# Power of the norms on few columns, low weight parts on VectorE, and operand sums of the weights kept in DRAM, in a hybrid decoder layer

## The chip, the cores and the metric

The kernel runs on one core of one Trainium2 chip. The metric is the device time of one execution in microseconds (us). In the rows of the profile PE is TensorE's matmuls, PEld its weight loads, DVE is VectorE, ACT ScalarE, POOL GpSimd, and SP (SPq) SyncE's queue, which here issues every DMA.

## The reference

One layer of a decoder runs over 2048 prompt tokens and 64 sample tokens. Two mixers (an S5 scan and an HGRN2 recurrence) give a row of 1024 numbers per token. What matters here comes behind them:

```python
def rmsnorm(x, g):
    xf = x.astype(jnp.float32)
    r = xf * lax.rsqrt(jnp.mean(xf * xf, axis=-1, keepdims=True) + EPS)
    return (r * g.astype(jnp.float32)).astype(x.dtype)
...
        x = x + jnp.concatenate([y5, yh], axis=-1) @ w_out[l]
        h2 = rmsnorm(x, norm_ffn[l])
        x = x + (jax.nn.silu(h2 @ w_gate[l]) * (h2 @ w_up[l])) @ w_down[l]
...
    y = rmsnorm(x, norm_final)
```

`w_out` is 1024 x 1024, `w_gate` and `w_up` are 1024 x 2816, `w_down` is 2816 x 1024, all in float32.

## The kernel before

The work falls into two parts. Up to about 842 us the mixers run (projections, the recurrence's heads, the scan, the gated unit). Behind that the 2112 tokens are taken in three blocks b = 0, 1, 2 of FT = 704, each in two halves of FH = 352: `mix` multiplies by `w_out` (matmuls into `pA_o`, `pB_o`, `pQ_o`), `norm2` normalises and stores the combinations of h that the next product needs, `ffn` runs the gate/up steps and then the down products, and `final` normalises the result and stores it. The order of the stages is mix 0, mix 1 with norm2 of block 0 in its middle, mix 2 with norm2 of block 1, norm2 of block 2, ffn 0, ffn 1 with the last norm of block 0 set behind its second step, ffn 2 with that of block 1, and the last norm of block 2 alone at the end. The norms are named f0, f1, f2 (`norm2`) and z0, z1, z2 (`final`).

Every large product is a two-by-two block product made with seven multiplications instead of eight, which `seven` issues. Each wants a sum of blocks of the weights as stationary data and one of the tokens as moving data. An operand is a float32 sum split in two parts, hi (its rounding, `wh`, `xh`) and lo (the rest, `wl`, `xl`), and three matmuls of 128 x 352 replace one: hi hi, lo hi, hi lo. So a gate/up step, which makes two pairs of blocks of 128 columns of gate and of up, is 7 products x 2 matrices x 12 = 168 matmuls. There are 11 such steps per block, and 6 groups of down products with 924 matmuls per block.

`w_prep` makes the weights' operands for one step: for each matrix it loads 1 MB in two DMAs of 512 KB into a raw tile `wr` (two of them exist), makes four sums of the four blocks on DVE (L1037, L1038, L1044, L1045), and for each of the seven operands lets ACT write hi (L1031) and POOL write lo (L1032). The seven operands go to a pool of ten slots, so a slot must be freed by the matmuls of an earlier operand. All weights are read and summed again in each of the three blocks.

A gate/up product ends in a sink: for gate `s` gets the product by ACT, or DVE adds a second product (L1105) and ACT takes SiLU; for up DVE adds (L1128) and multiplies `s` by `u` (L1129); the last up product is multiplied (L1119), DVE makes four combinations `T` (L976 to L979), and seven stores of 176 KB write `s_s`. The gate's last product (the seventh, at the 145th matmul of the step) goes to the bank of `pA_g`, and waits for L1105 to have read that bank.

`norm_r` squares eight tiles of 128 x 704 on ACT, adds them on DVE, sums over the partitions by a matmul with a matrix of ones (L1174), which gives each sum on all 128 partitions, scales on DVE (L1175), and raises to the power -1/2 on POOL over 128 x 704 (L1176). `norm2` and `final` then multiply on DVE (L1185, L1201).

The order of instructions on each engine is fixed when the program is built, by a scheduler that plans with its own costs. An engine runs its list in order, so an instruction that waits holds those behind it.

Of the kernel before, what the change touches and what calls it, by code (L numbers as in the profile page):

```python
# [265 lines left out]
def tiles_of(t0, n):  # L266
    r = []
    while n > 0:
        w = min(P, n)
# [20 lines left out]
        nc.gpsimd.tensor_tensor(r[:rows, a:b], st[:rows, a:b], e.mhalf[:rows, 0:b - a], op=ALU.pow)  # L290


def spread(e, r, tiles, name):
# [717 lines left out]
    return out  # L1011


def w_prep(e, mats, nk):
# [4 lines left out]
    out = [[] for _ in mats]
    gens = []  # L1020

    def prep(srcs, name, ops):
# [24 lines left out]
        sp(a12)
        yield
        sp(a21)
        yield  # L1050
        sp(a22)
        yield
# [403 lines left out]
```

## Time and profile before

| | |
|---|---|
| runs | 3363.42, 3372.87, 3374.15 us |
| median | 3372.87 us |
| profiled execution | 3370.24 us |
| its span, first to last instruction | 3368.5 us |
| granted TensorE clock, mean | 0.861 of full speed |
| PE, DVE, ACT, POOL busy | 2398.2, 2269.8, 996.7, 2300.7 us |

Three engines are busy for two thirds of the span, and none for all of it. So a share over the whole span does not say what holds the kernel; the stages have to be looked at one by one.

### The profile page before, as it was taken

To read this page: it belongs to the slowest core of one execution; us is meant where nothing else is said; L and a number is where in the kernel's file an instruction comes from. 1 tells how busy PE (TensorE), PEld (TensorE's weight loads), DVE (VectorE), ACT (ScalarE), POOL (GpSimd) and SP (SyncE) were. 2 spreads that over 40 slices of the span, in tenths; PEclk is the share of its full clock that TensorE was granted. 3 is DMA by queue.
4 is the path that set the end of the run, shared out by engine and by line. 5 is a ranking of instruction groups with operands and counts; after the bars stand their busy time and mean duration, and the time that the engine had idled before them with its cause. 6 is when DMAs were issued, how large, how long until landed. Compare 5 with 4: busy or idle time off the path is not lost.

```text
span 3368.5 us, 44865 instructions
## 1 busy us (share of the span) xinstructions
PE 2398.2 (71%) x16813; PEld 2210.8 (66%) x16813; DVE 2269.8 (67%) x2692; ACT 996.7 (30%) x1848; POOL 2300.7 (68%) x1587
## 2 busy tenths in 40 slices
PE   7989999997713705029999985298998816898840
PEld 6977677785703705029998985288988816898840
DVE  8754545455596896946678788667777795667730
ACT  4322222222301302004434442043434402344310
POOL 4176585511587698866667778976767797666778
PEclk9999999998856857559999998599999957999975
DMA  8865644545414704123324431142353204334300
GB/s 253 226 226 163 182 152 144 161 141 194 162 59 149 258 16 143 57 83 125 138 100 159 142 138 47 68 166 104 138 176 131 99 4 167 114 118 156 131 19 34
DMA packets 249323, 441.57 MB, mean 131 GB/s; under 512 B 80265, under 2 KB 165586, under 8 KB 249106
## 3 DMA queue, kind: packets, MB, share of 16 engines
q1 hardware_dynamic: 249106, 438.71, 39.1%
q8 instruction: 132, 2.16, 0.3%
q14 instruction: 85, 0.70, 0.1%
HBM read 314.86 MB, written 123.76 MB: 130 GB/s over the span
## 4 chain that ended last, share of the span: by engine, by line
PE 30%; DVE 21%; POOL 19%; DMA 12%; issue 10%; POOLq 3%; ACT 2%; SPq 1%; DVEq 0%; ACTq 0%
POOL rr_f L1176 7%; PE pA_u L1076 4%; POOLq L1448 3%; POOL rr_z L1176 3%; PE pA_g L1076 3%; DMA wr_u<-in_w_up_u 3%; PE pA_d L1076 3%; DVE ct L976 2%; DMA wr_wd<-in_w_down_u 2%; POOL wl_wd L1032 2%; PE ps_v L263 2%; PE ps_u L263 2%; DVE s L1129 2%; PE ps_f L263 1%; PE pQ_g L1076 1%
## 5 line engine op out<-in xcount | busy, mean ns | idle before, releaser
L1032 POOL TENSOR_TENSOR wl_u<-wr_u,wh_u 128x512 fp32r<-128x512 f32 x231 | 354.9, 1541 | 198.5 <-ACT wh_u L1031 154.6
L1032 POOL TENSOR_TENSOR wl_wd<-wr_wd,wh_wd 128x512 fp32r<-128x512 f32 (+1 forms) x252 | 382.7, 1545 | 151.9 <-ACT wh_wd L1031 137.8
L1032 POOL TENSOR_TENSOR wl_g<-wr_g,wh_g 128x512 fp32r<-128x512 f32 x231 | 353.0, 1531 | 140.4 <-ACT wh_g L1031 136.2
L1176 POOL TENSOR_TENSOR rr_z<-rr_z,mhalf 128x704 f32<-128x704 f32 x3 | 338.0, 112665 | 18.5 <-DVE rr_z L1175 18.5
L1176 POOL TENSOR_TENSOR rr_f<-rr_f,mhalf 128x704 f32<-128x704 f32 x3 | 337.9, 112625 | 10.9 <-DVE rr_f L1175 10.9
L1076 PE MATMUL pA_g<-xh_h,wh_g 128*128 128x352 f32 x528 | 186.1, 352 | 220.5 <-ACT s L1103 137.2
L1076 PEld LDWEIGHTS pA_g<-xh_h,wh_g 128*128 128x128 f32 x528 | 107.1, 203 | 231.7 <-ACT s L1103 138.1
L1076 PE MATMUL pA_g<-xh_h,wl_g 128*128 128x352 f32 x528 | 182.1, 345 | 98.8 <-POOL wl_g L1032 98.8
L1076 PE MATMUL pA_o<-xh_y,wh_wo 128*128 128x352 f32 x192 | 73.2, 385 | 247.3 <-ACT xh_y L1008 117.3
L1076 PE MATMUL pA_u<-xh_h,wh_u 128*128 128x352 f32 x528 | 178.7, 338 | 85.3 <-ACT u L1126 72.7
L1032 POOL TENSOR_TENSOR wl_wo<-wr_wo,wh_wo 128x512 fp32r<-128x512 f32 x84 | 143.1, 1731 | 109.2 <-ACT wh_wo L1031 100.2
L1076 PE MATMUL pA_d<-xh_s,wh_wd 128*128 128x352 f32 x528 | 179.7, 340 | 44.3 <-DVE acc_d L1091 44.1
L1076 PEld LDWEIGHTS pA_o<-xh_y,wh_wo 128*128 128x128 f32 x192 | 43.3, 227 | 254.3 <-ACT xh_y L1008 118.9
L1031 ACT ACTIVATE wh_wd<-wr_wd 128x512 fp32r<-128x512 f32 (+1 forms) x252 | 140.5, 588 | 221.7 <-DMA wr_wd<-in_w_down_u 97.7
L1129 DVE TENSOR_TENSOR s<-s,u 128x352 f32<-128x352 f32 x99 | 183.0, 1849 | 11.9 <-ACT s L1106 6.1
L1031 ACT ACTIVATE wh_g<-wr_g 128x512 fp32r<-128x512 f32 x231 | 143.1, 624 | 150.9 <-DMA wr_g<-in_w_gate_u 69.8
L1031 ACT ACTIVATE wh_u<-wr_u 128x512 fp32r<-128x512 f32 x231 | 143.0, 625 | 149.7 <-DMA wr_u<-in_w_up_u 47.7
L1076 PE MATMUL pA_g<-xl_h,wh_g 128*128 128x352 f32 x528 | 180.5, 342 | 0.0
L1106 ACT ACTIVATE s<-s 128x352 f32<-128x352 f32 x99 | 49.2, 497 | 431.7 <-DVE s L1105 430.9
L1076 PE MATMUL pA_d<-xh_s,wl_wd 128*128 128x352 f32 x528 | 176.1, 334 | 0.0
L1076 PE MATMUL pA_d<-xl_s,wh_wd 128*128 128x352 f32 x528 | 176.0, 333 | 0.0
L1076 PE MATMUL pA_u<-xh_h,wl_u 128*128 128x352 f32 x528 | 175.2, 332 | 0.5 <-POOL wl_u L1032 0.5
(495 smaller groups left out, 8546.6 us busy)
## 6 DMA issues: line engine op xcount, KB each, us to landing
wr_g<-in_w_gate_u SPq DMA_DIRECT2D x66, 512.0 KB, 4.5
wr_u<-in_w_up_u SPq DMA_DIRECT2D x66, 512.0 KB, 5.8
xr_s<-s_s SPq DMA_DIRECT2D x42, 704.0 KB, 4.3
wr_wd<-in_w_down_u SPq DMA_DIRECT2D x48, 512.0 KB, 5.7
s_s<-T SPq DMA_DIRECT2D x132, 176.0 KB, 1.8
s_s<-s SPq DMA_DIRECT2D x99, 176.0 KB, 1.9
xr_h<-h_s SPq DMA_DIRECT2D x21, 704.0 KB, 4.4
wr_wo<-in_w_out_u SPq DMA_DIRECT2D x24, 512.0 KB, 7.2
```

The source lines that it names most:

```text
L263: e.nc.tensor.matmul(out, whl[k][a], xhl[k][b], start=start and i == 0, stop=stop and i == len(seq) - 1)
L976: v.tensor_tensor(t[0], b12, b11, op=ALU.subtract)
L1031: nc.scalar.activation(hi, src, AF.Copy)
L1032: nc.gpsimd.tensor_tensor(lo, src, hi.bitcast(F32), op=ALU.subtract)
L1076: nc.tensor.matmul(ps, W[i][w][:, ks], X[i][x][:, k], start=first and k == 0 and c == 0, stop=i in (1, 4, 6) and k == nk - 1 and c == 2, s ...
L1106: nc.scalar.activation(s[w], s[w], AF.Silu)
L1129: v.tensor_tensor(s[w], s[w], u[w], op=ALU.mult)
L1176: nc.gpsimd.tensor_tensor(r, r, e.mhalf[:, 0:1].to_broadcast([P, FT]), op=ALU.pow)
L1448: with tile.TileContext(nc, schedule_with_timeline_sim=True) as tc:
```

## The change

Three things change. In `norm_r` the sums over the partitions are made by matmuls whose moving data is one column of ones, so that 128 tokens' sums lie on 128 partitions in one column: three matmuls of one column for each half, scale and power on 128 x 2 and 96 x 1, then a diagonal matrix of the results (as the first norm of the kernel does already) and three matmuls with ones that spread it over the partitions again, and an ACT copy to `r`. In `w_prep` lo is made by DVE, not POOL. And the four sums of a matrix are made in block 0 only; they are stored (1 MB) to DRAM, and in blocks 1 and 2 loaded from there: 512 KB of two blocks, 1 MB of four sums, 256 KB of a third block in place of 1 MB.

```diff
+def diagonal(e, r, tiles, name):
+    dg = e.diag.tile([P, 4, P], F32, tag="dg", name=f"dg_{name}")
+    for rows, a, b in parts_of(tiles):
+        nc.vector.tensor_tensor(dg[:rows, a:b], e.ident[:rows, None, :].to_broadcast([rows, b - a, P]),
+                                r[:rows, a:b, None].to_broadcast([rows, b - a, P]), op=ALU.mult)
+    return dg
...
-        raw = e.wraw.tile([P, 6, 512], F32, tag="wr", name=f"wr_{name}")
-        for fh in range(2):
-            nc.sync.dma_start(raw[:, 2 * fh:2 * fh + 2, :n], srcs[fh].rearrange("p (h f) -> p h f", h=2))
-        a11, a12, a21, a22, s1, s2 = (raw[:, i, :n] for i in range(6))
+        raw = e.wraw.tile([P, 7, 512], F32, tag="wr", name=f"wr_{name}_{b}")
+        if b == 0:
+            e.sum_s[name] = e.dr.tile([P, 4, 512], F32, name=f"sum_{name}")
+        keep = e.sum_s[name][:, :, :n]
+        src = [x.rearrange("p (h f) -> p h f", h=2) for x in srcs]
+        nc.sync.dma_start(raw[:, 0:2, :n], src[0])
+        if b == 0:
+            nc.sync.dma_start(raw[:, 5:7, :n], src[1])
+        else:
+            nc.sync.dma_start(raw[:, 2:6, :n], keep)
+            nc.sync.dma_start(raw[:, 6, :n], src[1][:, 1])
+        a11, a12, s1, s2, s4, s3, a22 = (raw[:, i, :n] for i in range(7))
...
-            nc.gpsimd.tensor_tensor(lo, src, hi.bitcast(F32), op=ALU.subtract)
+            v.tensor_tensor(lo, src, hi.bitcast(F32), op=ALU.subtract)
...
-        v.tensor_tensor(s1, a21, a22, op=ALU.add)
-        v.tensor_tensor(s2, s1, a11, op=ALU.subtract)
+        if b == 0:
+            v.tensor_tensor(s1, s3, a22, op=ALU.add)
+            v.tensor_tensor(s2, s1, a11, op=ALU.subtract)
...
+        if b == 0:
+            v.tensor_tensor(s4, a12, s2, op=ALU.subtract)
+            v.tensor_tensor(s3, a11, s3, op=ALU.subtract)
+            nc.sync.dma_start(keep, raw[:, 2:6, :n])
         sp(s2)
-        v.tensor_tensor(a12, a12, s2, op=ALU.subtract)
-        v.tensor_tensor(a21, a11, a21, op=ALU.subtract)
...
-        hs = slice(h * FH, h * FH + FH)
-        ps = e.psN.tile([P, 512], F32, tag="n", name=f"ss_{name}_{h}")[:, :FH]
-        nc.tensor.matmul(ps, e.ones, tot[:, hs], start=True, stop=True)
-        nc.vector.tensor_scalar(r[:, hs], ps, 1.0 / D, EPS, op0=ALU.mult, op1=ALU.add)
-    nc.gpsimd.tensor_tensor(r, r, e.mhalf[:, 0:1].to_broadcast([P, FT]), op=ALU.pow)
+        o = h * FH
+        tl = tiles_of(0, FH)
+        ss = e.psN.tile([P, 512], F32, tag="n", name=f"ss_{name}_{h}")
+        for j, (c, w) in enumerate(tl):
+            nc.tensor.matmul(ss[:w, j:j + 1], tot[:, o + c:o + c + w], e.ones[:, 0:1], start=True, stop=True)
+        rc = e.small.tile([P, 4], F32, tag="r", name=f"r_{name}_{h}")
+        inv_rms(e, ss, tl, rc, f"{name}_{h}")
+        dg = diagonal(e, rc, tl, f"{name}_{h}")
+        pr = e.psN.tile([P, 512], F32, tag="n", name=f"pr_{name}_{h}")
+        for j, (c, w) in enumerate(tl):
+            nc.tensor.matmul(pr[:, c:c + w], e.ones[:w], dg[:w, j, :w], start=True, stop=True)
+        nc.scalar.activation(r[:, o:o + FH], pr[:, :FH], AF.Copy)
```

The lists of instructions of all five engines are the same before and after up to the start of the mix stage. Three places behind it follow. The names are those of the tiles with the program's numbers behind them; `wr_g_2` is the raw tile of gate weights in block 2.

DVE in ffn of block 2, the step with the sinks `s_17` (step 10 of 11) while the weights of the next step are prepared; first before:

```order
L1037 TENSOR_TENSOR wr_u_2_24187<-wr_u_2_24187 128x512 [waits DMAHW7_49,Pool_49]
L1038 TENSOR_TENSOR wr_u_2_24187<-wr_u_2_24187 128x512 [waits DMAHW6_49,DVE_49]
L1045 TENSOR_TENSOR wr_u_2_24187<-wr_u_2_24187 128x512
L1044 TENSOR_TENSOR wr_g_2_24180<-wr_g_2_24180 128x512 [waits Pool_49]
L1105 TENSOR_TENSOR s_17_2_24066<-s_17_2_24066,pB_g_2_24024 128x352 [waits DMAHW2_49,PE_49,Activation_49]
L1044 TENSOR_TENSOR wr_u_2_24187<-wr_u_2_24187 128x512 [waits DVE_49,Pool_49]
L1128 TENSOR_TENSOR u_17_2_24080<-u_17_2_24080,pB_u_2_24039 128x352 [waits DMAHW5_49,PE_49,Activation_49]
L1129 TENSOR_TENSOR s_17_2_24066<-s_17_2_24066,u_17_2_24080 128x352 [waits DVE_49,Activation_49]
L976 TENSOR_TENSOR T_17_2_24165<-s_17_2_24066,s_17_2_23977 128x352 [waits DMAHW0_49,DVE_49]
L1105 TENSOR_TENSOR s_17_2_24037<-s_17_2_24037,pA_g_2_23964 128x352 [waits PE_49]
```

and the same stretch after, where L1047 makes lo, L1120 is L1105 of before and L1143, L1144 are L1128, L1129:

```order
L1144 TENSOR_TENSOR s_17_2_24012<-s_17_2_24012,u_17_2_24027 128x352 [waits DVE_49]
L1047 TENSOR_TENSOR wl_g_2_0_24220<-wr_g_2_24215,wh_g_2_0_24219 128x512 [waits DMAHW7_49,PE_49,Activation_49]
L1047 TENSOR_TENSOR wl_u_2_0_24228<-wr_u_2_24223,wh_u_2_0_24227 128x512 [waits DMAHW2_49,PE_49,Activation_49]
L1047 TENSOR_TENSOR wl_g_2_1_24232<-wr_g_2_24215,wh_g_2_1_24231 128x512 [waits PE_49,Activation_49]
L1047 TENSOR_TENSOR wl_u_2_1_24236<-wr_u_2_24223,wh_u_2_1_24235 128x512 [waits PE_49,Activation_49]
L1120 TENSOR_TENSOR s_17_2_24101<-s_17_2_24101,pB_g_2_24059 128x352 [waits DMAHW6_49,PE_49]
L1047 TENSOR_TENSOR wl_g_2_2_24240<-wr_g_2_24215,wh_g_2_2_24239 128x512 [waits DMAHW0_49,Activation_49]
L1143 TENSOR_TENSOR u_17_2_24115<-u_17_2_24115,pB_u_2_24074 128x352 [waits DMAHW1_49,PE_49]
L1047 TENSOR_TENSOR wl_u_2_2_24244<-wr_u_2_24223,wh_u_2_2_24243 128x512 [waits DMAHW4_49,Activation_49]
L1144 TENSOR_TENSOR s_17_2_24101<-s_17_2_24101,u_17_2_24115 128x352 [waits DVE_49]
L982 TENSOR_TENSOR T_17_2_24200<-s_17_2_24101,s_17_2_24012 128x352 [waits DVE_49]
L1120 TENSOR_TENSOR s_17_2_24072<-s_17_2_24072,pA_g_2_23999 128x352 [waits PE_49]
```

The sums in front of the sink of `pA_g` are gone, and six lo instructions of the next step stand there, the last two of which (operand 2) read the sums loaded from DRAM.

SP's queue at the same step, before:

```order
L1025 DMA wr_g_2_24180<-in_w_gate_u 128x1024 [waits DMAHW3_49,Pool_49]
L1025 DMA wr_g_2_24180<-in_w_gate_u 128x1024 [waits DMAHW4_49]
L1123 DMA s_s_2_81<-s_17_2_23977 128x352 [waits DMAHW5_49,DVE_49]
L1025 DMA wr_u_2_24187<-in_w_up_u 128x1024 [waits DMAHW6_49,Pool_49]
L1025 DMA wr_u_2_24187<-in_w_up_u 128x1024 [waits DMAHW7_49]
```

and after:

```order
L1035 DMA wr_g_2_24215<-in_w_gate_u 128x1024 [waits DMAHW7_49,DVE_49]
L1039 DMA wr_g_2_24215<-sum_g_14610 128x2048 [waits DMAHW0_49]
L1040 DMA wr_g_2_24215<-in_w_gate_u 128x512 [waits DMAHW1_49]
L1035 DMA wr_u_2_24223<-in_w_up_u 128x1024 [waits DMAHW2_49,DVE_49]
L1138 DMA s_s_2_81<-s_17_2_24012 128x352 [waits DMAHW3_49,DVE_49]
L1039 DMA wr_u_2_24223<-sum_u_14618 128x2048 [waits DMAHW4_49]
L1040 DMA wr_u_2_24223<-in_w_up_u 128x512 [waits DMAHW5_49]
```

Four loads of 2 MB became six of 3.5 MB, and their start waits for DVE's last lo of the step before, where it waited for POOL's.

PE's last instructions, those of the norm z2, before:

```order
L1174 MATMUL ss_z_0_26096<-sum_z_26072,ones 128x352 [waits DVE_49]
L1174 MATMUL ss_z_1_26099<-sum_z_26072,ones 128x352 [waits DVE_49]
```

and after:

```order
L1191 MATMUL ss_z_0_26089<-ones,sum_z_26065 128x1 [waits DVE_49,PE_49]
L1191 MATMUL ss_z_0_26089<-ones,sum_z_26065 128x1
L1191 MATMUL ss_z_0_26089<-ones,sum_z_26065 96x1
L1197 MATMUL pr_z_0_26102<-dg_z_0_26099,ones 128x128 [waits DVE_49,PE_49]
L1197 MATMUL pr_z_0_26102<-dg_z_0_26099,ones 128x128
L1197 MATMUL pr_z_0_26102<-dg_z_0_26099,ones 128x96 [waits DVE_49]
L1191 MATMUL ss_z_1_26107<-ones,sum_z_26065 128x1 [waits Activation_49]
L1191 MATMUL ss_z_1_26107<-ones,sum_z_26065 128x1
L1191 MATMUL ss_z_1_26107<-ones,sum_z_26065 96x1
L1197 MATMUL pr_z_1_26120<-dg_z_1_26117,ones 128x128 [waits DVE_49,PE_49]
L1197 MATMUL pr_z_1_26120<-dg_z_1_26117,ones 128x128
L1197 MATMUL pr_z_1_26120<-dg_z_1_26117,ones 128x96 [waits DVE_49]
```

The second half's sums wait for the ACT copy of the first half, since both use one PSUM bank.

## Rows read from the trace of the kernel before

**Rows 1.** The page, costliest groups: busy us, mean ns of one | idle before, releaser.

```profile
L1032 POOL TENSOR_TENSOR wl_u<-wr_u,wh_u 128x512 fp32r<-128x512 f32 x231 | 354.9, 1541 | 198.5 <-ACT wh_u L1031 154.6
L1176 POOL TENSOR_TENSOR rr_z<-rr_z,mhalf 128x704 f32<-128x704 f32 x3 | 338.0, 112665 | 18.5 <-DVE rr_z L1175 18.5
L1176 POOL TENSOR_TENSOR rr_f<-rr_f,mhalf 128x704 f32<-128x704 f32 x3 | 337.9, 112625 | 10.9 <-DVE rr_f L1175 10.9
```

**Rows 2.** Timeline of the end: start, length, engine, line, [idle before <-releaser].

```profile
3241.70 0.86 PE L1174 MATMUL ss_z<-sum_z,ones 128*128 128x352 f32 x2 [3.41 <-DVE sum_z L1169]
...
3245.43 112.47 POOL L1176 TENSOR_TENSOR rr_z<-rr_z,mhalf 128x704 f32<-128x704 f32 x1 [18.50 <-DVE rr_z L1175]
3357.94 6.99 DVE L1201 SCALAR_TENSOR_TENSOR acc_d<-acc_d,gain,rr_z 128x704 f32<-128x704 f32 x8 [112.65 <-POOL rr_z L1176]
```

**Rows 3.** Timeline around the norms f0 and f2.

```profile
952.53 80.26 DVE L976 TENSOR_TENSOR ct<-cy 128x352 f32<-128x352 f32 x1 [1.99 <-DMA cy<-y_s]
...
1064.51 0.95 PE L1076 MATMUL pA_o<-xh_y,wh_wo 128*128 128x352 f32 x2 [114.53 <-ACT xh_y L1008]
...
1496.73 0.66 PE L1076 MATMUL pA_g<-xh_h,wh_g 128*128 128x352 f32 x1 [135.96 <-ACT s L1103]
```

**Rows 4.** Windows: from:to, length, busy (instructions) PE PEld DVE ACT POOL, PEclk, DMA share, GB/s.

```profile
1175.00:1290.00 115.00, 15.15 (x75) 14.33 (x74) 87.20 (x16) 7.66 (x12) 114.30 (x3) 0.57 0.07 27
1290.00:1362.00 72.00, 48.91 (x244) 44.00 (x242) 66.22 (x65) 24.05 (x33) 50.24 (x30) 0.85 0.65 229
...
1520.00:1798.00 278.00, 257.88 (x1549) 255.28 (x1548) 191.40 (x203) 115.69 (x223) 187.83 (x129) 0.97 0.34 121
...
2065.00:2180.00 115.00, 21.37 (x103) 20.79 (x102) 87.09 (x11) 3.41 (x8) 115.00 (x7) 0.57 0.06 20
2180.00:2430.00 250.00, 225.35 (x1318) 220.92 (x1317) 177.32 (x186) 102.30 (x197) 170.83 (x115) 0.95 0.40 144
2430.00:2603.00 173.00, 155.16 (x924) 151.65 (x922) 130.77 (x152) 74.83 (x111) 124.26 (x83) 0.97 0.42 146
...
2805.00:3063.00 258.00, 231.49 (x1366) 227.21 (x1365) 179.01 (x190) 107.23 (x203) 175.40 (x119) 0.95 0.41 148
3063.00:3245.00 182.00, 161.89 (x943) 157.28 (x941) 133.23 (x162) 68.03 (x105) 119.27 (x79) 0.95 0.34 115
```

**Rows 5.** Timeline of PE in one gate/up step of block 1.

```profile
2261.78 0.33 PE L1076 MATMUL pQ_g<-xh_h,wh_g 128*128 128x352 f32 x1
...
2270.70 0.32 PE L1076 MATMUL pA_g<-xh_h,wl_g 128*128 128x352 f32 x1
...
2288.78 0.66 PE L1076 MATMUL pA_g<-xh_h,wh_g 128*128 128x352 f32 x1 [4.73 <-DVE s L1105]
...
2292.17 0.49 PE L1076 MATMUL pA_g<-xh_h,wl_g 128*128 128x352 f32 x1
```

**Rows 6.** Who waited for line 1105 (us, times), whole trace.

```profile
  PE pA_g L1076: 77.9, 29
```

**Rows 7.** Groups of DVE in 2200 to 2430 us, shapes apart: busy us, mean ns.

```profile
L1044 DVE TENSOR_TENSOR wr_g<-wr_g 128x512 f32<-128x512 f32 x8 | 13.4, 1669 | 0.0
...
L1105 DVE TENSOR_TENSOR s<-s,pA_g 128x352 f32<-128x352 f32 x7 | 3.6, 509 | 0.0
```

**Rows 8.** Timeline of DVE late in the power f1 (1175.7 to 1288.2 us).

```profile
1258.67 0.69 DVE L1045 TENSOR_TENSOR wr_wo<-wr_wo 128x512 f32<-128x512 f32 x1
```

**Rows 9.** Timeline of the kernel's first norm, on 128 x 2.

```profile
10.80 0.58 DVE L289 TENSOR_SCALAR st_u<-ssr_u 128x2 f32<-128x2 f32 x1 [9.93 <-ACT xr_u L312]
...
11.52 0.70 POOL L290 TENSOR_TENSOR rcol<-st_u,mhalf 128x2 f32<-128x2 f32 x1 [0.17 <-DVE hgn L194]
...
14.00 1.26 DVE L338 SCALAR_TENSOR_TENSOR r_xu<-r_xu,gain,rr_u 128x256 f32<-128x256 f32 x3 [0.22 <-PE rr_u L301]
```

**Rows 10.** DMA from 2839.5 to 2847 us, 40 slices: weights of one step.

```profile
GB/s 153 218 175 393 437 284 371 262 306 437 415 459 371 415 459 219 240 175 197 175 350 393 503 350 415 393 262 437 371 328 350 350 284 197 88 22 22 0 0 0
DMA packets 577, 2.11 MB, mean 282 GB/s; under 512 B 64, under 2 KB 64, under 8 KB 576
```

More of the change, by code (lines that the diff above doesn't have):

```diff
@@ L290, in inv_rms @@
         nc.gpsimd.tensor_tensor(r[:rows, a:b], st[:rows, a:b], e.mhalf[:rows, 0:b - a], op=ALU.pow)
-def spread(e, r, tiles, name):
+def diagonal(e, r, tiles, name):
     nc = e.nc
@@ L298, in spread @@
                                 r[:rows, a:b, None].to_broadcast([rows, b - a, P]), op=ALU.mult)
+    return dg
+def spread(e, r, tiles, name):
+    nc = e.nc
+    dg = diagonal(e, r, tiles, name)
     pr = e.ps_x.tile([P, 512], F32, tag="x", name=f"rr_{name}")
@@ L1011, in x_slots, with w_prep @@
     return out
-def w_prep(e, mats, nk):
+def w_prep(e, mats, nk, b):
     nc = e.nc
@@ L1019, in w_prep @@
     out = [[] for _ in mats]
-    gens = []
     def prep(srcs, name, ops):
-        raw = e.wraw.tile([P, 6, 512], F32, tag="wr", name=f"wr_{name}")
-        for fh in range(2):
-            nc.sync.dma_start(raw[:, 2 * fh:2 * fh + 2, :n], srcs[fh].rearrange("p (h f) -> p h f", h=2))
-        a11, a12, a21, a22, s1, s2 = (raw[:, i, :n] for i in range(6))
+        raw = e.wraw.tile([P, 7, 512], F32, tag="wr", name=f"wr_{name}_{b}")
[10 more added lines that the diff above has]
+        a11, a12, s1, s2, s4, s3, a22 = (raw[:, i, :n] for i in range(7))
         def sp(src):
             ws = e.ws.pick()
-            hi, lo = (ws.tile([P, 512], F32R, tag="w" + c, name=f"w{c}_{name}_{len(ops)}")[:, :n] for c in "hl")
+            hi, lo = (ws.tile([P, 512], F32R, tag="w" + c, name=f"w{c}_{name}_{b}_{len(ops)}")[:, :n] for c in "hl")
             nc.scalar.activation(hi, src, AF.Copy)
-            nc.gpsimd.tensor_tensor(lo, src, hi.bitcast(F32), op=ALU.subtract)
+            v.tensor_tensor(lo, src, hi.bitcast(F32), op=ALU.subtract)
             ops.append((hi, lo))
@@ L1042, in prep @@
         yield
+        if b == 0:
+            v.tensor_tensor(s4, a12, s2, op=ALU.subtract)
+            v.tensor_tensor(s3, a11, s3, op=ALU.subtract)
+            nc.sync.dma_start(keep, raw[:, 2:6, :n])
         sp(s2)
-        v.tensor_tensor(a12, a12, s2, op=ALU.subtract)
-        v.tensor_tensor(a21, a11, a21, op=ALU.subtract)
         yield
[L1047 to L1052, printed above, removed]
+        for x in (s4, s3, a22):
+            sp(x)
+            yield
     gens = [prep(srcs, name, ops) for (srcs, name), ops in zip(mats, out)]
@@ L1148, in mix @@
         js = (2 * g, 2 * g + 1)
-        W = w_prep(e, [([e.i["w_out_u"][d] for d in (j, j + 4)], f"wo{j}_{b}") for j in js], 4)
+        W = w_prep(e, [([e.i["w_out_u"][d] for d in (j, j + 4)], f"wo{j}") for j in js], 4, b)
         mats = [(w, acc_sink(e, x[j], x[j + 4]), f"o{j}_{b}") for w, j in zip(W, js)]
@@ L1211, in ffn @@
             nm = f"{f[0]}_{b}"
-            W = w_prep(e, [([e.i["w_gate_u"][i] for i in f], "g" + nm), ([e.i["w_up_u"][i] for i in f], "u" + nm)], 4)
+            W = w_prep(e, [([e.i[w][i] for i in f], f"{n}{f[0]}") for w, n in (("w_gate_u", "g"), ("w_up_u", "u"))], 4, b)
             mats = [(W[0], gate_sink(e, s, nm), "g" + nm), (W[1], up_sink(e, s, nm, e.s_s[b][c], j), "u" + nm)]
@@ L1222, in ffn @@
             js = (2 * g, 2 * g + 1)
-            W = w_prep(e, [([e.i["w_down_u"][d][:, cs] for d in (j, j + 4)], f"wd{j}_{b}_{c}") for j in js], nk)
+            W = w_prep(e, [([e.i["w_down_u"][d][:, cs] for d in (j, j + 4)], f"wd{j}_{c}") for j in js], nk, b)
             mats = [(w, acc_sink(e, x[j], x[j + 4]), f"d{j}_{b}_{c}") for w, j in zip(W, js)]
@@ L1254, in body @@
     e.ro_s = dr.tile([4, P, 8, 16], F32, name="ro_s")
+    e.dr, e.sum_s = dr, {}
     e.x1_s = dr.tile([D, TOK], F32, name="x1_s")
```

## The prediction

> **What bounds the kernel now.** The page's costliest groups come first. Two of them stand out by the length of one instruction: the power on 128 x 704 takes POOL 112.7 us each time, six times, 676 us in all, a fifth of the time [rows 1]. Whether that is paid depends on what waits, so the timeline of each of the six comes next. The last one (z2) is plain: from the ones-matmul at 3241.7 to the first multiplication at 3357.9, 116.2 us, nothing else runs [rows 2]. For the others the windows show what PE still does: in the 115 us around f1 75 matmuls, around z0 103, at a granted clock of 0.57, and about 20 us of PE work in all [rows 4]; z1 is as z0, with 103. Around f2 PE is idle for 135.96 us, before it the 114.53 us of f0 [rows 3]. Two things are late in each: what needs the norm, and everything that needs DVE, because a DVE instruction with two SBUF operands that starts under the power stands for some 80 us (a subtraction of 128 x 352 took 80.26 us) [rows 3].
>
> The second question is the pace of the products between the norms. Undisturbed, 57 matmuls start from 2261.78 to 2270.70 us, 0.16 us apart [rows 5], so a step of 168 could take 26.9 us. The windows give 278/1549 x 168 = 30.2 us in block 0, 31.9 in block 1, 31.7 in block 2; the down products go at 0.187 and 0.193 us a matmul [rows 4]. The step in the timeline shows where it goes: at the seventh gate product PE waits 4.73 us for DVE's sink L1105, and then twelve matmuls need 3.4 us up to the last start, at 0.5 us each instead of 0.32: they run at the lower of the two clock levels after the wait [rows 5]. Over the trace PE waits 77.9 us there, in 29 of 33 steps [rows 6], 2.7 us each, and the slow twelve cost 1.6 more. DVE is late since its SBUF work is stretched: a sum of 128 x 512 took 1.67 us in the mean, beside 0.69 for one alone; the sinks that read PSUM kept their 0.51 [rows 7, 8]. The stretch is about one lo of POOL, 1.54 us [rows 1].
>
> **The norms.** A half now needs, one behind the other, three column matmuls, scaling, power, diagonal, three matmuls, ACT's copy. The kernel's first norm has this chain on 128 x 2: 10.80 to 14.00 us, 3.2 us, with a power of 0.70 [rows 9]. Added here are the column matmuls (as the two ones-matmuls of 0.86 [rows 2]), a second small scale, power and diagonal for the 96 remaining tokens (about 1.2, from 0.70 and two short DVE operations), and the copy (about 0.5, as a sink of that shape [rows 7]): some 5.7 us. One PSUM bank makes the halves follow each other: 11.4 us. Nothing in the trace has a matmul with one column; I price it like the ones shown, and between nothing and twice that the norm moves by 2 us.
> - z2: 116.2 - 11.4 = 105 saved.
> - f2: of 135.96 idle, 112.6 is the power; the products of h and their stores behind it stay. 112.6 - 11.4 - 4 for DVE work of the first ffn step that mixes in: 97.
> - z0, z1: 115 - 103 x 0.19 = 95, less 1 for the chain, whose two halves lie under 34 to 37 matmuls (5.5 us) each: 94 each. Those matmuls are the cover; without it each norm would cost 11.
> - f1: 115 - 75 x 0.295 (the pace of the mix behind it, 72/244 [rows 4]) = 93, less 1: 92.
> - f0: 80.26 of the stalled subtraction go. The remaining combinations of y up to PE's restart at 1064.51 stay, and the list after puts norm2's multiplications and stores of block 0 ahead of the combinations, for which I take 10: 70.
>
> Sum 552. If a wait is worth less than it seems, it is f0, down to nothing where the loads of y hold PE; the other five are empty stretches of one cause.
>
> **lo on DVE.** 798 instructions of POOL (wl_u is one of four such groups) become DVE instructions of 0.69 us [rows 1, 8], and nothing on POOL stretches DVE any longer. Counted per gate/up step: in block 0 14 lo + 8 sums at 0.69 and 14 sinks and combinations at 0.51 give 22.3 us of 26.9; in blocks 1 and 2, without sums, 16.8. In a down group there are 14 sinks and, at half a chunk, 3.5 lo parts of tokens (128 x 1408, by length 1.9 us each): 28.9 of 26.9 in block 0, 23.4 later. So DVE fits except in the down products of block 0, where I take 5 us off in all (ends: 0 and 25, the excess of block 1). For block 0's gate/up steps, the sums still stand ahead of the sink that PE waits for, unstretched: about a third of the 36 us above PE's pace, 13 (ends 0 and 36).
>
> The Trainium skill, "Perfetto Trace Analysis", section "Optimizing Scalar/DVE Operations", says that work may be worth offloading from a saturated DVE, to GpSimd too, though the port they share might undo it. That speaks against the move: added to DVE's 2269.8 busy us, 798 x 0.69 = 551 would make 2821, above this forecast. By the rows the count goes the other way, since about 400 of the busy us are five stands of some 80 us under the power, as the one shown [rows 3], and much of the rest is stretched; the first rival below is what that section would lead to.
>
> **Sums from DRAM.** Blocks 1 and 2 save four sums per matrix, and load 1.75 MB instead of 1 MB. What this risks is a late load: DVE's list now has six lo of the next step ahead of the sink that frees the bank of `pA_g`, the last two from the stored sums; the loads start when DVE has made the last lo of the step. By the order that is at about the 48th matmul, 7.7 us; PE wants the bank at the 145th, 23.0 us. The hi, the lo and four sinks and combinations behind the load take 0.6 + 0.69 + 4 x 0.51 = 3.3 us, so 12.0 us are left for 3.25 MB (3.41 million bytes): 284 GB/s. One step's 2 MB moved at 282 GB/s in the mean from issue to quiet, start and end included, with 350 and more in many slices [rows 10]. So it just fits, with little to spare; ACT's hi wait in the same way. I take a step of 28.2 us: 26.9 and 1.3 for late loads. That is 40 us less for 11 steps in block 1 and 39 in block 2 (ends: 55 and 53 at PE's pace, below nothing with rates under 215 GB/s: 15.9 us, 3.9 late and 1.6 of slow clock, 32.4 us). The down products of block 1 and 2, 173 and 182 us against 148 at 0.16, get back 15 and 18 (ends 0 and 25, 34). The mix stages of block 1 and 2 run at 229 GB/s already [rows 4], with more to load now, but with DVE relieved: 10 (ends -10 and 35). The stores of sums in block 0 (1 MB per matrix) are waited for by the raw tile's next load; DMA is busy there at 0.34 [rows 4], so I price them at nothing, and at 11 to 22 us if each step's load came 1 to 2 us later on the path.
>
> Sum: 13 + 40 + 39 + 5 + 15 + 18 + 10 = 140.
>
> **Rivals.**
> - DVE takes POOL's place as what PE waits for. For it: one in-order list holds lo, sinks and waits for loads, and 284 GB/s is needed at once; against it: the counts above. Then the 140 are not there: 3370.2 - 552 = 2818.
> - PE's pace everywhere from the ffn on: 36 + 55 + 53 + 25 + 25 + 34 = 228, and 20 in the mix. For it: blocks 1 and 2 lose both sums and stretch; against it: block 0's counts. 3370.2 - 552 - 248 = 2570.
> - Late loads cost more than the stretch did: at 200 GB/s under the stores the step goes to 17.0 us of load, 33.5 us, 1.7 more than now, and the down groups alike: 34 steps x 1.5 = 50: about 2868.
> - The powers are not what holds, and the time on few columns is that of a call: then each of the 24 small powers would cost as much as a large one. The 0.70 us of the first norm speaks against it [rows 9]. It would be no faster, about 3370.
> - The other side, slower than before: only the loads of stored sums reach so far. To eat 552 us, 38 preparation steps (22 gate/up, 12 down, 4 mix) must each be 14.5 us above today: 46.3 us, so 17.8 late, 29.8 us for 3.41 MB, 114 GB/s. The stage now moves 144 to 148 GB/s in the mean with DMA busy at 0.40 [rows 4]. From that point on it decides; at 100 GB/s it gives some 3530.
>
> **The numbers.** Profiled execution 3370.2 - 552 - 140 = 2678; the execution lies 2.7 us under the median of the runs (3372.87), so 2680. Chances: the forecast 0.60 (its own range 2630 to 2740), PE's pace everywhere 0.15, no gain from the preparation 0.15, a loss there 0.06, powers that don't shrink 0.02, slower 0.02. The range goes from 2575 to 2825: it holds the forecast and the greater part of the two cases next to it. The runs before spread over 0.32%, so about 0.3%, 10 us, is what can be told from no change. Faster than that 0.97, within it 0.01, slower 0.02.
>
> **What would show it.** The end from the last column matmuls to the first multiplication: 10 to 13 us. No DVE instruction of tens of us. PE idle at f2 near 40 us, and no 100 us stretch under a granted clock of 0.6. DVE's 128 x 512 instructions at 0.7 us. Windows of gate/up: 29 us a step in block 0, 28 in blocks 1 and 2. I am wrong by the sum if the wait of PE for the gate's sink (L1120 now) stays at 2.7 us a step, with DVE or ACT waiting for the DMA of the sums in front of it; if it goes away wholly, the time is nearer to 2600.

## The result, and the profile after

The changed kernel takes 2526.18 us (median of 4 runs, 2524.53 to 2532.38) beside 3368.14 us for the kernel before: a ratio of 0.7504, 95% interval 0.7482 to 0.7526. The forecast was 2680 us with a range from 2575 to 2825. The direction was right and the gain was larger than the range allowed, by 49 us at its lower end and by 154 us against the forecast. One execution of a kernel below, that with the norm and lo alone, took 10712.32 us, for a reason that no run shows; its ratio and interval leave it out, and the median of its other three is 2537.19 us.

The page of the kernel after, its first parts: busy time, and PE's busy tenths and granted clock in 40 slices.

```profile
PE 2313.9 (92%) x16933; PEld 2162.1 (86%) x16933; DVE 1700.1 (67%) x3222; ACT 1013.0 (40%) x1860; POOL 416.4 (16%) x807
...
PE   6999999999998463975999999999999999999997
...
PEclk9999999999999786987999999999999999999998
```

One engine is now busy nearly all the time. The dips that are left lie in the mix stages, at a third of the span; from slice 20 on PE is full at the full clock, up to the last norm in the last slice. POOL has lost 1884 us of work and DVE 570, although 798 lo parts were added to it; the sums of two blocks and the long stands under the powers have left it.

The end, timeline of the kernel after, answers to [rows 2]:

```profile
2503.53 0.75 PE L1191 MATMUL ss_z<-ones,sum_z 128*128 128x1 f32 x6 [3.50 <-DVE sum_z L1184]
2504.31 0.22 DVE L289 TENSOR_SCALAR st_z<-ss_z 128x2 f32<-128x2 f32 x2 [0.93 <-PE ss_z L1191]
2504.61 1.22 POOL L290 TENSOR_TENSOR r_z<-st_z,mhalf 128x2 f32<-128x2 f32 x2 [388.33 <-DVE st_z L289]
2505.35 0.81 DVE L297 TENSOR_TENSOR dg_z<-consts,r_z 128x256 f32<-128x256 f32 x2 [0.82 <-POOL r_z L290]
...
2507.53 0.46 ACT L1198 ACTIVATE rr_z<-pr_z 128x352 f32<-128x352 f32 x1 [5.32 <-PE pr_z L1197]
2508.04 1.33 PE L1191 MATMUL ss_z<-ones,sum_z 128*128 128x1 f32 x6 [0.55 <-ACT rr_z L1198]
...
2513.11 6.99 DVE L1223 SCALAR_TENSOR_TENSOR acc_d<-acc_d,gain,rr_z 128x704 f32<-128x704 f32 x8 [1.86 <-ACT rr_z L1198]
```

From the column matmuls to the first multiplication it is 9.6 us (11.4 were forecast), in two halves of 4.5 and 5.1 us; the second starts when the copy of the first has freed the bank. Six column matmul records take 0.75 us.

Windows of the kernel after, cut at the last matmul of each stage: gate/up and down of blocks 0, 1 and 2. Columns as in [rows 4].

```profile
1131.40:1462.50 331.10, 300.28 (x1842) 298.74 (x1841) 247.23 (x433) 147.76 (x272) 2.81 (x4) 0.94 0.60 217
1462.50:1612.90 150.40, 149.97 (x936) 149.69 (x936) 140.01 (x236) 74.29 (x111) 0.00 (x0) 1.00 0.68 245
1612.90:1908.00 295.10, 295.10 (x1849) 295.10 (x1848) 189.53 (x336) 147.73 (x273) 2.96 (x4) 1.00 0.60 220
1908.00:2058.50 150.50, 149.85 (x936) 149.01 (x935) 116.67 (x192) 73.26 (x111) 0.00 (x0) 1.00 0.62 224
2058.50:2356.40 297.90, 297.90 (x1866) 297.90 (x1865) 191.16 (x335) 149.38 (x276) 3.63 (x4) 1.00 0.60 220
2356.40:2499.70 143.30, 143.30 (x899) 143.30 (x898) 107.55 (x179) 62.28 (x95) 0.00 (x0) 1.00 0.52 187
```

In blocks 1 and 2 PE is busy 100% of the gate/up stages at 0.1597 us a matmul, 26.8 us a step. Two norms lie inside these windows and leave no gap. In the down products of block 0, where the forecast had DVE overfull, PE is busy for 149.97 of 150.40 us.

### The profile page after: what moved, and what is told of

Read it like the earlier page. It is cut to its first block, busy times and chain, and to the rows that moved or that the text cites. A ratio compares the mean times of both kernels' runs of the same rounds, so it can differ in the third digit from the quotient of the medians.

```text
span 2523.7 us, 44154 instructions
## 1 busy us (share of the span) xinstructions
PE 2313.9 (92%) x16933; PEld 2162.1 (86%) x16933; DVE 1700.1 (67%) x3222; ACT 1013.0 (40%) x1860; POOL 416.4 (16%) x807
## 4 chain that ended last, share of the span: by engine, by line
PE 70%; DMA 10%; DVE 9%; POOL 7%; issue 2%; ACT 2%; SPq 1%; DVEq 0%; ACTq 0%; POOLq 0%
PE pA_u L1091 10%; PE pA_g L1091 10%; PE pA_d L1091 8%; PE pB_u L1091 5%; PE pB_g L1091 5%; PE pB_d L1091 4%; PE ps_v L263 3%; PE ps_u L263 3%; PE pQ_g L1091 3%; PE pQ_u L1091 2%; PE pQ_d L1091 2%; PE ps_f L263 2%; PE pz L263 2%; DMA cy<-y_s 2%; PE ps_q L263 2%
## 5 line engine op out<-in xcount | busy, mean ns | idle before, releaser
L1047 DVE TENSOR_TENSOR wl_g<-wr_g,wh_g 128x512 fp32r<-128x512 f32 x231 | 158.6, 687 | 114.2 <-ACT wh_g L1046 112.6
L1047 DVE TENSOR_TENSOR wl_u<-wr_u,wh_u 128x512 fp32r<-128x512 f32 x231 | 158.7, 688 | 98.5 <-ACT wh_u L1046 97.6
L1046 ACT ACTIVATE wh_u<-wr_u 128x512 fp32r<-128x512 f32 x231 | 144.3, 628 | 151.3 <-DMA wr_u<-in_w_up_u 39.5
L1091 PE MATMUL pA_g<-xh_h,wh_g 128*128 128x352 f32 x528 | 172.9, 328 | 30.7 <-ACT s L1118 22.9
L1091 PE MATMUL pA_g<-xh_h,wl_g 128*128 128x352 f32 x528 | 172.6, 327 | 6.0 <-DVE wl_g L1047 6.0
L1091 PE MATMUL pA_d<-xh_s,wh_wd 128*128 128x352 f32 x528 | 170.3, 323 | 0.4 <-DVE acc_d L1106 0.4
L1091 PE MATMUL pA_u<-xl_h,wh_u 128*128 128x352 f32 x528 | 169.5, 321 | 0.0
L1047 DVE TENSOR_TENSOR wl_wd<-wr_wd,wh_wd 128x512 fp32r<-128x512 f32 (+1 forms) x252 | 156.9, 641 | 16.5 <-ACT wh_wd L1046 16.4
L1091 PEld LDWEIGHTS pA_g<-xh_h,wh_g 128*128 128x128 f32 x528 | 100.4, 190 | 31.8 <-ACT s L1118 23.4
L504 DVE TENSOR_TENSOR q<-q,tot 128x256 f32<-128x256 f32 (+1 forms) x96 | 53.0, 552 | 95.2 <-PE p L477 34.5
L1091 PEld LDWEIGHTS pA_g<-xh_h,wl_g 128*128 128x128 f32 x528 | 100.7, 191 | 6.3 <-DVE wl_g L1047 6.3
L1015 DVE TENSOR_TENSOR xl_s<-xr_s,xh_s 128x1408 fp32r<-128x1408 f32 (+1 forms) x63 | 94.4, 1499 | 11.1 <-ACT xh_s L1014 10.6
```

What stands on the lines that cost most here:

```text
L504: vec.tensor_tensor(qv[:, :, 1], qv[:, :, 1], t[:, :, 0:1].to_broadcast(shp), op=ALU.mult)
L1015: nc.vector.tensor_tensor(lo, raw, hi.bitcast(F32), op=ALU.subtract)
L1047: v.tensor_tensor(lo, src, hi.bitcast(F32), op=ALU.subtract)
L1091: nc.tensor.matmul(ps, W[i][w][:, ks], X[i][x][:, k], start=first and k == 0 and c == 0, stop=i in (1, 4, 6) and k == nk - 1 and c == 2, s ...
```

## The experiments

**Which of the three edits brings what.** Four kernels carry one or two of the edits: the norm alone, lo on DVE alone, norm with lo, norm with stored sums. Their edit is the function of before or after as a whole, and for lo one line:

```diff
-            nc.gpsimd.tensor_tensor(lo, src, hi.bitcast(F32), op=ALU.subtract)
+            v.tensor_tensor(lo, src, hi.bitcast(F32), op=ALU.subtract)
```

Norm alone. 

> The norms on few columns alone, weights prepared as before (lo on POOL, sums in every block). Theory 1 (the forecast's sum: the norms are worth 552 us, the preparation 140): 3368 - 552 = 2816 us. Theory 2 (the norms were undervalued, and the missing 150 us lie in the mix stages that waited behind the powers): about 2670. In both no DVE instruction of tens of us; in theory 1 PE still waits about 2.7 us a step for the gate's sink and DVE's sums of 128 x 512 stay at 1.3 to 1.7 us.

Lo on DVE alone. 

> Lo on DVE alone, powers on 128 x 704 kept, sums made in every block. Theory 1 (DVE as full as the forecast counted it: 22.3 us of 26.9 in a gate/up step, 28.9 of 26.9 in a down group): no gain, 3340 to 3390 us. Theory 2 (what held the steps was the stretch alone, and with POOL quiet DVE keeps up even with the sums): gate/up and down of all three blocks at 0.160 to 0.163 us a matmul, 220 us less, and as much again is not given back by the powers: 3130 to 3170.

Norm and lo. 

> Norms on few columns and lo on DVE, sums made in every block (nothing kept in DRAM). Theory 1 (the stored sums are needed, since DVE with 22.3 us of sums, lo and sinks a step is late for the gate's sink): blocks 1 and 2 at 28 to 29 us a step and 0.18 us a matmul in the down products, 2610 to 2640 us. Theory 2 (the stretch alone was the cost): as block 0 of the changed kernel in all blocks, 0.1624 us a matmul in gate/up, 2526 + 2 x 5 = 2536, or lower where the mix stages load less.

Norm and stored sums. 

> Norms on few columns and sums kept in DRAM, lo still on POOL. Theory 1 (stretch by POOL is what makes DVE late, also without the sums): blocks 1 and 2 keep about half their excess over PE's pace, 2640 to 2700 us. Theory 2 (taking the eight sums off DVE is enough in blocks 1 and 2, only block 0 keeps its old pace of 0.18): 2526 + 32 + 25 + some 10 in the mix = 2590. POOL's lo stay at 1.3 to 1.5 us, 21 us of 26.9 a step.

| norm on few columns | lo on DVE | sums stored | median us | ratio to before, 95% interval |
|---|---|---|---|---|
| - | - | - | 3373.96 | 1 |
| yes | - | - | 2759.93 | 0.8174 (0.8149 to 0.8200) |
| - | yes | - | 3092.58 | 0.9168 (0.9133 to 0.9203) |
| yes | - | yes | 2650.04 | 0.7852 (0.7830 to 0.7875) |
| yes | yes | - | 2538.67 | 0.7523 (0.7501 to 0.7544) |
| yes | yes | yes (once more, later) | 2527.93 | 0.7519 (0.7495 to 0.7543) |

The norm is worth 614 us by itself, lo on DVE 221 on top of it, and stored sums on top of both nothing that the intervals can tell apart (0.7523 and 0.7519). With lo still on POOL the stored sums bring 110 us, so the two preparation edits are two cures for one thing. Of the expectations, theory 2 held for norm with lo (2536 expected, 2539 found), and for lo alone in the pace of the down products (149.7 us in block 0, 0.162 a matmul), while its range was missed (3093, below the 3130 to 3170); for the norm alone the result lies between the theories, 56 us below the one and 90 above the other; for norm with stored sums theory 1's 2640 to 2700 holds, though the gate/up stages of blocks 1 and 2 kept only 17 and 11 us of their 48 and 45 above the kernel after, where it had expected about half.

The lengths of the stages by trace, in us, each from the last matmul of the stage before to its own last matmul (the first two from the first product of mix):

| stage | before | norm | norm, lo | after |
|---|---|---|---|---|
| mix of all blocks, norms f0, f1 | 502.7 | 309.9 | 285.8 | 282.9 |
| gate/up 0 with f2 | 469.7 | 367.5 | 332.8 | 331.1 |
| down 0 | 173.9 | 174.7 | 151.3 | 150.4 |
| gate/up 1 with z0 | 453.5 | 343.3 | 299.0 | 295.1 |
| down 1 | 177.4 | 174.8 | 143.8 | 150.5 |
| gate/up 2 with z1 | 449.0 | 342.6 | 305.1 | 297.9 |
| down 2 | 163.7 | 166.8 | 141.8 | 143.3 |
| end with z2 | 130.5 | 24.0 | 24.0 | 24.0 |

The column on lo shows something on the power, too. With lo on DVE and the powers kept, gate/up 1 took 374.3 us (from 1918.6 to 2292.9), 75 more than the 299.0 without the powers; with lo on POOL the same norm costs 453.5 - 343.3 = 110. Of the 35 us between, 23.4 show as one wait of PE for POOL, which makes a lo part only behind the power; the rest was not taken apart. Waits of PE in gate/up 1 before, then with lo on DVE (us, times, longest):

```profile
PE pA_u L1076 <- ACT u L1126: 71.5, 2, 70.2
...
PE pB_g L1076 <- POOL wl_g L1032: 23.4, 1, 23.4
```

```profile
PE pB_u L1082 <- ACT u L1132: 75.1, 1, 75.1
```

**Is it POOL's reading, or POOL's lateness?** In the kernel after, a subtraction is added on POOL for each lo; it reads hi, and nothing reads its result:

```diff
             v.tensor_tensor(lo, src, hi.bitcast(F32), op=ALU.subtract)
+            nc.gpsimd.tensor_tensor(e.junk[:, :n], hi.bitcast(F32), hi.bitcast(F32), op=ALU.subtract)
```

> The changed kernel with 798 subtractions more on POOL, one beside each lo of DVE, of the same shape, which read hi from SBUF and whose result nobody uses. Theory 1 (POOL's reading of SBUF by itself stretches DVE, and that was the loss of the products before): DVE's lo go from 0.69 to above 1.3 us, the list of DVE gets longer than PE's 26.9 us a step, and all of the 221 us that lo on DVE brought are gone: 2740 us or more. Theory 2 (PE waited because lo came late out of POOL's list, 1.5 us each): nothing waits for POOL now, 2526 to 2545.

It took 2823.12 us (2 runs, ratio 0.8370, 0.8349 to 0.8390): 297 us are lost to work whose result nobody reads. Groups of DVE from 1900 to 2250 us in this kernel, shapes apart, and PE's waits over the whole trace (us, times, longest):

```profile
L1047 DVE TENSOR_TENSOR wl_u<-wr_u,wh_u 128x512 fp32r<-128x512 f32 x45 | 47.0, 1046 | 25.5 <-ACT wh_u L1046 19.6 <-PE pB_u L1092 5.8
...
L1107 DVE TENSOR_TENSOR acc_d<-acc_d,pA_d 128x352 f32<-128x352 f32 x36 | 18.2, 509 | 1.1 <-PE pA_d L1092 1.1
```

```profile
PE pA_g L1092 <- DVE s L1121: 79.2, 26, 5.3
...
PE pA_d L1092 <- DVE acc_d L1107: 40.0, 29, 4.0
```

DVE's lo went from 0.69 to 1.05 us in the mean (above 1.3 had been expected), the sink that reads PSUM kept 0.51, and PE waits for DVE's sinks again, 79.2 us for the gate's alone, as in the kernel before [rows 6]. POOL itself is waited for a little: ACT waits 24.3 us in all for it, 8 times, since a slot of hi is free only when POOL has read it. So POOL's work beside DVE is enough to make it late, as theory 1 has it; the added instructions also write to SBUF, and no run parts their reading from their writing. In this kernel DVE makes lo as well, so it doesn't tell by itself what the kernel with lo on POOL waited for. The trace with the norm alone, where POOL makes lo and no power stands in its way, does. PE's waits there, whole trace:

```profile
PE pA_g L1082 <- DVE s L1111: 70.5, 30, 5.6
PE pA_d L1082 <- DVE acc_d L1097: 47.5, 28, 4.4
...
PE pQ_d L1082 <- POOL wl_wd L1038: 1.4, 2, 0.7
...
PE pQ_g L1082 <- POOL wl_g L1038: 1.3, 1, 1.3
```

PE's waits for a lo of POOL come to 3.6 us in all, those for the two groups of DVE's sinks above to 118.0. And one of DVE's sums in gate/up of block 1, with the norm alone and with lo on DVE as well:

```profile
L1051 DVE TENSOR_TENSOR wr_u<-wr_u 128x512 f32<-128x512 f32 x9 | 15.5, 1727 | 0.0
```

```profile
L1051 DVE TENSOR_TENSOR wr_u<-wr_u 128x512 f32<-128x512 f32 x10 | 6.8, 682 | 0.0
```

The same instruction takes 1.73 us beside POOL's lo and 0.68 without them. So what the products lost was DVE time taken by POOL's work on SBUF beside it, and hardly the lateness of POOL's results; behind a power that lateness does count, as the wait of 23.4 us above shows.

**Do the loads of the sums fit?** The forecast had taken 1.3 us a step for late loads. First 512 KB were copied from DRAM to DRAM ahead of each load:

```diff
+            nc.sync.dma_start(e.dr.tile([P, 2, 512], F32, name=f"sp_{name}_{b}")[:, :, :n], keep[:, 0:2])
             nc.sync.dma_start(raw[:, 2:6, :n], keep)
```

> The changed kernel with more DMA work in front of every load of stored sums in blocks 1 and 2: a copy of 512 KB from DRAM to DRAM whose result nobody reads, per matrix, 2.1 MB more moved per step. Theory 1 (the forecast's account of the load: 12.0 us for 3.41 MB, nearly used up): with 1.05 MB more ahead of the last load the bank of the gate's product is freed 1.5 us too late, 1.6 more for slow matmuls, in 22 steps and half as much in the down groups: 2600 us or more. Theory 2 (the load has several us to spare, which is why the forecast's 1.3 us a step did not come): within 15 us of 2526, PE busy all through the windows of blocks 1 and 2.

2563.43 us (0.7601, 0.7587 to 0.7615), but this answers another question: nothing ties the copies to their step, and the planned list set them into block 0, right behind the stores of the sums. There they cost 4 us in mix, 11 in gate/up and some 14 in the down products; 12 of the 42 us by which its span is longer lie ahead of the mix stage, and what made them stays open. In blocks 1 and 2 PE waited 0.7 us in all. So the same question was asked with a load into the raw tile, which has to wait for that tile:

```diff
+            nc.sync.dma_start(raw[:, 2:4, :n], keep[:, 0:2])
             nc.sync.dma_start(raw[:, 2:6, :n], keep)
```

> The changed kernel where half of each matrix's stored sums (512 KB) is loaded first and then all four sums (1 MB) over them, so 4.46 MB instead of 3.41 MB stand ahead of the last sums of a step in blocks 1 and 2 (the copies of the earlier run could move ahead of the block and did). Theory 1 (the forecast's account of 12.0 us was about right, and the changed kernel has just the 1 us that its trace shows between the bank being freed and PE's need): 1.05 MB at 330 GB/s is 3.2 us, so 2.2 late and 1.6 of slow matmuls, 3.8 us in 22 steps, and half of that in 12 down groups: 2610 to 2640 us. Theory 2 (the lists of ACT, DVE and PE shift and take it up): 2526 to 2545.

2545.57 us (0.7569, 0.7546 to 0.7591), 18 us above the run of the kernel after beside it, where the account of 12.0 us asked for 84 and more. In block 1 PE stays busy while DMA moves 256 to 264 GB/s, by the windows of this kernel in gate/up and down:

```profile
1605.00:1900.00 295.00, 294.03 (x1843) 293.45 (x1843) 195.13 (x338) 145.68 (x274) 2.98 (x4) 1.00 0.71 256
1900.00:2050.00 150.00, 149.80 (x938) 149.48 (x937) 111.99 (x184) 70.20 (x110) 0.00 (x0) 1.00 0.72 264
```

The list of DVE says how. In it the lo of the up matrix's first stored sum now stands behind the gate's sink, where it stood ahead of it:

```order
L1121 TENSOR_TENSOR s_17_2_24134<-s_17_2_24134,pA_g_2_24061 128x352 [waits PE_49]
L1048 TENSOR_TENSOR wl_u_2_2_24308<-wr_u_2_24286,wh_u_2_2_24307 128x512 [waits DMAHW5_49,DMAHW3_49,Activation_49]
```

The scheduler plans with the load, so by this list a later load moves the instruction that needs it, and not the sink, for which PE never waits here. In gate/up of block 2, which takes 11 us more than in the kernel after, PE does wait twice for a hi part of the up weights whose load was late:

```profile
2066.87 0.43 PE L1092 MATMUL pA_u<-xh_h,wh_u 128*128 128x352 f32 x1 [2.45 <-ACT wh_u L1047]
...
2165.32 0.43 PE L1092 MATMUL pB_u<-xh_h,wh_u 128*128 128x352 f32 x1 [1.71 <-ACT wh_u L1047]
```

What the rest of these 11 us is stays open. Theory 2 holds, at the upper end of its range and for this size of load; what a load does that is later than planned was not tried.

**A better order.** The longest waits of PE that are left are for operands of mix. This moves the combinations of y for block 2 behind the first half of mix of block 1:

```diff
-        for b in (1, 2):
-            combine_y(e, b, Cmb(e))
+        combine_y(e, 1, Cmb(e))
...
             norm2(e, b - 1, got[b - 1]["x"])
+            if b == 1:
+                combine_y(e, 2, Cmb(e))
             run(mg)
```

> The changed kernel with the combinations of y for block 2 made behind the first half of mix of block 1 instead of ahead of mix of block 1. Theory 1 (the empty stretch of PE from 935 to 1000 us is the chain of eight loads and combinations, four of which block 2 alone needs): 25 to 30 us less, about 2498. Theory 2 (the stretch is bound by the stores of h and the loads of the accumulators on the same queue): 2520 to 2530.

Without stored sums: 

> As the run with the later combinations, and the sums made in every block (nothing kept in DRAM). Theory 1 (keeping the sums is worth about nothing once DVE is quick): within 8 us of that run. Theory 2 (keeping the sums is worth the 12 us seen between the kernels without and with it): 10 to 15 us above it.

Ahead of the norm: 

> As the run with the later combinations, but these stand ahead of the norm of block 0 instead of behind it. Theory 1 (the norm's stores on SP's queue were what took back half of the gain): 8 to 15 us below 2515. Theory 2 (what is left is the loads themselves): 2510 to 2520.

The repeat beside it: 

> The changed kernel once more, timed beside the two others: 2526 us within 0.3%.

They took 2515.12 us (0.7457, 0.7443 to 0.7471), 2526.64 us (0.7477, 0.7459 to 0.7495) and 2512.42 us (0.7468, 0.7448 to 0.7487); the repeat of the kernel after took 2527.93 us. The later combinations gain 11 to 16 us, half of what was expected, and the place beside the norm makes no difference that shows (the last of the three, 2510 to 2520 expected). Waits of PE from 840 to 1170 us, after and with the later combinations:

```profile
PE pA_o L1091 <- ACT xh_y L1014: 47.2, 2, 45.4
```

```profile
PE pA_o L1091 <- ACT xh_y L1014: 25.9, 4, 20.7
```

The longest wait halved. What is left fits the loads themselves, which no run took apart: between the two mix stages, 1009.9 to 1044.7 us in this kernel, PE did 5.5 us of work while DMA ran at 311 GB/s. These versions are the fastest that were run. Storing the sums makes 11 us of difference in them by the medians, as theory 2 had it, but the intervals with and without overlap, so it is not decided between the two theories.

## Why the forecast was wrong

The mechanisms of the forecast held: the powers were empty stretches, POOL's lo parts were what made DVE late, and no DVE instruction of tens of us is left. The sizes failed, in two terms of the sum, and both on the same side.

**The preparation: 140 forecast, 234.5 us measured** (spans 2758.2 with the norm alone and 2523.7 after). By stage, forecast and measured: mix 10 and 27, gate/up 13, 40, 39 and 36, 48, 45, down 5, 15, 18 and 24, 24, 24; 6 more lie ahead of the mix. The step that failed is what I let DVE still cost PE once nothing stretched it: only "about a third of the 36 us" given back in gate/up of block 0, because the sums still stand ahead of the sink; "28.9 of 26.9" in its down products; 1.3 us a step for late loads in blocks 1 and 2. The runs gave nearly all of it back: in the kernel after PE waits for no sink of the gate at all, and for those of the down products twice, the longer wait being this one of the whole trace (us, times, longest).

```profile
PE pA_d L1091 <- DVE acc_d L1106: 0.4, 1, 0.4
```

The first of the three had no row behind it. The second was a count of DVE's time that added lengths of instructions. DVE's timeline in a step of block 2 after shows that the starts follow each other closer than that:

```profile
2208.78 0.68 DVE L1047 TENSOR_TENSOR wl_g<-wr_g,wh_g 128x512 fp32r<-128x512 f32 x1
2209.38 0.69 DVE L1047 TENSOR_TENSOR wl_u<-wr_u,wh_u 128x512 fp32r<-128x512 f32 x1
2209.98 0.68 DVE L1047 TENSOR_TENSOR wl_g<-wr_g,wh_g 128x512 fp32r<-128x512 f32 x1
2210.59 0.51 DVE L1143 TENSOR_TENSOR u<-u,pB_u 128x352 f32<-128x352 f32 x1
2211.89 0.69 DVE L1047 TENSOR_TENSOR wl_u<-wr_u,wh_u 128x512 fp32r<-128x512 f32 x1 [0.79 <-ACT wh_u L1046]
2212.50 0.52 DVE L1144 TENSOR_TENSOR s<-s,u 128x352 f32<-128x352 f32 x1
2212.94 0.51 DVE L1120 TENSOR_TENSOR s<-s,pA_g 128x352 f32<-128x352 f32 x1
```

Starts lie 0.60 us apart for 128 x 512, and 0.44 for 128 x 352, where the lengths are 0.69 and 0.51. For a lo of 1408 columns the next start is 1.54 us later, in a step of block 0:

```profile
1261.00 1.63 DVE L1015 TENSOR_TENSOR xl_s<-xr_s,xh_s 128x1408 fp32r<-128x1408 f32 x1 [0.74 <-ACT xh_s L1014]
1262.54 0.69 DVE L1047 TENSOR_TENSOR wl_g<-wr_g,wh_g 128x512 fp32r<-128x512 f32 x1
```

With 0.60, 0.44 and 1.54 the counts become 19.4 us for a gate/up step of block 0 and 24.8 for a down group: both fit into 26.9. And a busy DVE was taken for a late one: in the down products of block 0 it is busy for 140.01 of 150.40 us and PE does not wait.

The third, 1.3 us a step for late loads, was caution and not a reading. The account of the load itself was nearly right, 12.0 us: in the same step of block 2 the loads of the next weights are issued from 2198.57 us, ACT gets the sums at 2211.23, 12.7 us later, and the sink frees the bank at 2213.45.

```profile
2198.57 0.33 SPq L1035 DMA_DIRECT2D wr_g<-in_w_gate_u  x1
...
2200.90 0.43 SPq L1039 DMA_DIRECT2D wr_u<-sum_u  x1
```

```profile
2211.23 0.63 ACT L1046 ACTIVATE wh_u<-wr_u 128x512 fp32r<-128x512 f32 x1 [1.57 <-DMA wr_u<-sum_u]
```

```profile
2213.43 0.32 PE L1091 MATMUL pA_g<-xh_h,wh_g 128*128 128x352 f32 x1
...
2216.16 0.32 PE L1091 MATMUL pA_g<-xh_h,wh_g 128*128 128x352 f32 x1
```

What the account had wrong is when PE wants the bank. It puts the seventh gate product behind the twelve matmuls of up alone. In the built list of the kernel after, 24 to 45 matmuls stand between the sixth and the seventh gate product of a step, since the first products of the next step are set there, in banks of their own. The matmul at 2213.43 begins such a product; the seventh begins at 2216.16, 2.71 us behind the end of the sink. Over the 33 steps this margin is 1.17 us at least and 3.18 in the middle one, and 1.29 to 3.46 in block 0, where the sums stand ahead of the sink. So the loads have more room than the account gave them, and PE waits for this sink in no step.

**The norms: 552 forecast, 614 us measured.** z2 was right (105 forecast, 106.5 measured), and f2 nearly (97 and 102). So was f0: from the first product of mix to the restart of PE behind the power it is 216.4 us before (848.1 to 1064.51 [rows 3]) and 144.4 with the norm alone (from 854.7), 72 less where 70 was forecast. The restart there:

```profile
999.06 0.95 PE L1082 MATMUL pA_o<-xh_y,wh_wo 128*128 128x352 f32 x2 [37.73 <-ACT xh_y L1014]
```

z0 and z1 were 94 each, and measured 110 and 106; f1 was 92, and the rest of the mix stages gave 121. The step that failed is "115 - 103 x 0.19", and its like for f1: I took the windows of the powers for all that the powers cost, while the stages around them were still paying. With the norm alone changed, the gate/up of block 1 runs at 0.1816 us a matmul, where the window behind z0 had 0.1897 [rows 4]. The window of that kernel: from:to, length, PE busy (instructions), granted clock, DMA share, GB/s.

```profile
1760.00:2050.00 290.00, 264.74 (x1597) 0.97 0.40 143
```

8 ns over 1318 matmuls are 11 us of the 16 that z0 was short; the other 5 stay open. For f1 the matmuls of mix can be counted, 1008 in both traces. The 168 that span the power take 150.2 us before and 56.7 with the norm alone, 93.5 less where 92 was forecast. But the 420 ahead of them, from the restart on, take 15.3 us less as well, and the 84 behind them 12.0 less, and neither was in the sum. What PE waited for longer in them no run took apart.

**The rivals.** The one with PE's pace everywhere (0.15, 2570 us) is what happened in all products; its 248 for the preparation stands against 234.5, and the norms' 62 us bring it close to the measured time. The forecast named this case as its sign of being wrong: if the wait for the gate's sink goes away wholly, the time is nearer to 2600. That DVE would take POOL's place (0.15) and the loss through late loads (0.06) fell with the windows of blocks 1 and 2. The section of the Trainium skill on offloading ("Perfetto Trace Analysis", "Optimizing Scalar/DVE Operations") holds by its second half here: between DVE and GpSimd the place of the work matters through what they share. With lo moved to it on top of the norm, DVE has 798 instructions more and is busy for 1866.4 us, where it was 1877.2 with the norm alone.

## What to carry to other kernels

Before adding up what an engine's list takes, read the distance between starts of neighbours, not the length of one, and compare the sum with the stage it must fit; an engine that is busy at 93% of a stage need not be late. The price of a long instruction is not the window that it fills: undo it in one run, or compare the pace of the stages ahead of it and behind it with those of a kernel that never had one. When a wait for a bank is priced, count the matmuls that the built list puts in front of it, not those of the loop. And when two edits cure the same wait, as lo on DVE and stored sums did here, the second one adds little or nothing; a table of each alone and both together shows it in four runs.

## What the runs showed of the hardware

The power on 128 x 704 blocked a DVE instruction with two SBUF operands for most of its length, but not for all of it. In the kernel before, the power f1 ran from 1175.70 us for 112.47; DVE's timeline there:

```profile
1181.25 76.78 DVE L1037 TENSOR_TENSOR wr_wo<-wr_wo 128x512 f32<-128x512 f32 x1
1258.06 0.69 DVE L1038 TENSOR_TENSOR wr_wo<-wr_wo 128x512 f32<-128x512 f32 x1
```

It ended at 1258.03, 82.3 us after the power's start, and the next such instructions ran at their own 0.69 us beside the remaining 30 us of the power. The subtraction of 80.26 us under f0 [rows 3] ended at 1032.79, the same distance behind its power, which began at 950.62. The Trainium skill, "SBUF — State Buffer", section "SBUF: two separate sides", says that of a DVE instruction with two SBUF inputs and a GpSimd one that reads SBUF the first to start holds the ports that they share for its whole length; here the measurement differs for this operation. Why it is let go at that point no run here shows.
